# Seven products and an eighth two K-steps later: the sums over partitions of nine conditioning parts, pinned in TensorE's order

## The chip, the cores and the metric

The kernel runs on one core of one Trainium2 chip. The metric is the device time of one execution in microseconds (us), lower is better. The core has TensorE (PE in the profile's rows; PEld is its loading of the stationary operand), VectorE (DVE), ScalarE (ACT), GpSimd (POOL) and SyncE (SP, whose queue starts nearly all loads of weights). Each engine carries out its own instructions in a fixed order, and engines wait for each other through semaphores.

## What is computed

One inference step of a two-layer backbone on 128 context tokens and 128 latent tokens, with a width D of 2048. Layer 0 mixes differential attention and a two-way RWKV-7 scan, layer 1 is a Conformer convolution module, and each layer ends with a ConvFFN. What the change touches is the conditioning: before each block, shift, scale and gate vectors come from a product of the conditioning vector with a 2048 by 12288 matrix per layer.

```python
def adaln(cvec, w, b):
    return (jax.nn.silu(cvec) @ w + b)[:, None, :]

for l in range(DEPTH):
    sh1p, sc1p, g1p, sh2p, sc2p, g2p = jnp.split(adaln(c_ctx[None, :], w_ada[l], b_ada[l]), 6, axis=-1)
    sh1s, sc1s, g1s, sh2s, sc2s, g2s = jnp.split(adaln(c, w_ada[l], b_ada[l]), 6, axis=-1)
    hp = rmsnorm(xp, norm_g[l, 0]) * (1.0 + sc1p) + sh1p
    ...
    xp = xp + g1p * mp
    hp = rmsnorm(xp, norm_g[l, 1]) * (1.0 + sc2p) + sh2p
    xp = xp + g2p * conv_ffn(hp, w_up[l], w_ffn_dw[l], w_down[l])
```

The rows for the latent tokens (xs, hs) are the same with the other vectors.

## The kernel before

**The matrix products.** Activations stand with the channels on the 128 partitions and 256 tokens (both streams) on the free axis, each number split in a high and a low part. A weight matrix is loaded in pieces of 512 KB into one of seven buffers `raw` (`RAW_BUFS`), ACT copies the high part out of it (L192) and DVE or POOL subtracts to get the low part (L194), into one of four slots `wbt`. `gemm` (L235) then runs over groups of output columns and, in each, over K-steps of 128 rows; a K-step with four output tiles is 12 products of 128x128 by 128x256 (L252, L254, L255; L268 to L270 are the same in the last four K-steps of a product that ends a block). After each K-step `gemm` calls a function `fill`, which is where other work is put into the program's order.

**The conditioning** is a Python generator, `ada_gen` (L463), which goes through parts of 1024 columns; each call of `ada_step` takes it to its next `yield`. A part is done in one of two ways. `ada_pe` (L392) multiplies on TensorE: a load of 128 rows by 1024 columns (512 KB, L402) gives four products of 128x32 by 128x256 (L421), one for each quarter j of the columns, and each goes to its own 32 partitions of the tile `ada` (32j to 32j+31). A step of layer 1's parts is two loads and eight products, and a part has eight such steps. `ada_vec` (L426) is used for nine parts, those in `AS_VEC`: DVE multiplies each loaded row block with a scalar and adds it to `av` (L444 and L446), once for each stream s, 32 operations in 32 steps; three idle steps later eight small products with the constant `sel` (L454) sum `av` over the partitions, four quarters j for each of the two streams. Then DVE turns the result (L460), the bias is added (L473), and the part is finished.

**The order of the nine parts** is: layer 0 `g2` (two parts), layer 1 `sc1` (two), `sh1` (two), and `g1` part 0, begun in layer 0's ConvFFN; layer 1 `g2` (two parts) in layer 1's ConvFFN. The parts between them (`g1` part 1, `sc2`, `sh2` of layer 1) are done by `ada_pe` during the convolution block.

**How often steps are taken.** In the two ConvFFNs (`fill0`, `fill2`) a step is taken every second K-step after the sixteenth. Layer 0's ConvFFN has 176 + 88 + 176 + 80 = 520 K-steps, hence 252 steps. In the convolution block (`fill1`) a step is taken every fourth K-step: 32 in its first product (`p_p1`, 144 K-steps), some in the loop after it, 15 in its second product (`p_p2`, 64 K-steps). `ada_until` takes all the steps that are missing at once where a value is needed: for `sh2` of layer 1 that is after `p_p2`, ahead of the second norm of layer 1 (`modulated`, L562, whose instructions are L522, L537, L582, L585 and L587).

**What sets the order.** A scheduler with a simulated timeline puts the program's instructions in order on each engine. It may move an instruction ahead of others on its engine when its operands are ready earlier by its simulation; `tc.keep_in_program_order` takes an instruction out of that.

Of the kernel before, what the change touches and what calls it, by code (L numbers as in the profile page):

```python
# [82 lines left out]
def tile_step(ctx: ExitStack, tc: tile.TileContext, A):  # L83
    nc = tc.nc
    pe, dve, act, pool, sp = nc.tensor, nc.vector, nc.scalar, nc.gpsimd, nc.sync
# [32 lines left out]
    sel = const.tile([P, 2, 32], F32, name="sel")  # L118
# [7 lines left out]
    def bank():  # L126
        return psm[0].tile([P, 512], F32, tag="mm", name="mm")
# [298 lines left out]
    def ada_vec(l, nm, b0, nb):  # L426

        nw = nb * P
        c0 = SEG[nm] * D + b0 * P
        av = nrm_[0].tile([P, 2, 1024], F32, tag="av", name="av", bufs=1)  # L430

        def load(kt):
            raw = rawp.tile([P, 1024], F32, tag="raw", name="raw")
            sp.dma_start(out=raw, in_=A["w_ada"][l, kt * P:(kt + 1) * P, c0:c0 + nw])
            return raw

        nxt = load(0)
        yield
        for kt in range(KT):
            raw, nxt = nxt, (load(kt + 1) if kt < KT - 1 else None)  # L440
            for s in range(2):
                sc = silu_c[:, kt, s:s + 1]
                if kt == 0:
                    dve.tensor_scalar(out=av[:, s], in0=raw, scalar1=sc, scalar2=None, op0=ALU.mult)  # L444
                else:
                    dve.scalar_tensor_tensor(out=av[:, s], in0=raw, scalar=sc, in1=av[:, s], op0=ALU.mult, op1=ALU.add)  # L446
                yield
        for _ in range(3):
            yield
        ps = psa.tile([P, 256], F32, tag="ada", name="ada")  # L450
        for s in range(2):
            rv = av[:, s].rearrange("p (b j c) -> p j b c", j=4, c=32)
            for j in range(4):
                pe.matmul(ps[32 * j:32 * j + 32, 0:nb * 32], lhsT=sel[:, s], rhs=rv[:, j], start=(s == 0), stop=(s == 1))  # L454
        yield
        return ada_turn(ps, nb)

    def ada_turn(ps, nb):
        tr = adap.tile([P, 8, 32], F32, tag="atr", name="atr")
        dve.transpose(out=tr[:, 0:nb].rearrange("p b c -> p (b c)"), in_=ps[:, 0:nb * 32])  # L460
        return tr[:, 0:nb, 0:2]

    def ada_gen():  # L463
        for l, nm, part, parts, b0, nb in ada_order:
            si = SEG[nm]
            if (l, nm, part) in AS_VEC:
                tr = yield from ada_vec(l, nm, b0, nb)
            else:
                tr = yield from ada_pe(l, nm, b0, nb, 2 if l else 1)
            bias = V(f"b_ada{l}", si * KT + b0, nb)  # L470
            av = adaT[:, l * 6 + si, 2 * b0:2 * (b0 + nb)].rearrange("p (b s) -> p b s", s=2)
            eng = pool if l and nm in ("sc2", "sh2") else dve
            eng.tensor_tensor(out=av, in0=tr, in1=bias.unsqueeze(2).to_broadcast([P, nb, 2]), op=ALU.add)  # L473
            if nm in ("sc1", "sc2"):
                ni = 0 if nm == "sc1" else 1
                gvec = V("norm_g", (l * 2 + ni) * KT + b0, nb).unsqueeze(2).to_broadcast([P, nb, 2])
                ac = Acoef[:, l * 2 + ni, b0:b0 + nb]
                if eng is pool:
                    pool.tensor_scalar(out=ac, in0=av, scalar1=1.0, scalar2=None, op0=ALU.add)
                    pool.tensor_tensor(out=ac, in0=ac, in1=gvec, op=ALU.mult)  # L480
                else:
                    dve.scalar_tensor_tensor(out=ac, in0=av, scalar=1.0, in1=gvec, op0=ALU.add, op1=ALU.mult)
            ada_done.add((l, nm, part))
            if part == parts - 1:
                ada_done.add((l, nm))
            yield
# [971 lines left out]
    with ExitStack():  # L1458
# [15 lines left out]
        with scoped("startp", 1) as stp:  # L1474
# [6 lines left out]
            ps = bank()  # L1481
# [13 lines left out]
            with scoped("rowp", 1) as rowp:  # L1495
# [3 lines left out]
                for kt in range(0, KT, 2):  # L1499
                    ps = bank()  # L1500
# [13 lines left out]
        with scoped("nrm1", 2) as nrm_[0]:  # L1514
# [76 lines left out]
            with scoped("cv", 1) as cvp, scoped("cvt", 2) as cvt:  # L1591
# [108 lines left out]
                ps = bank()  # L1700
                first = True
                for ct in list(range(C0, KT)) + [-1]:
# [6 lines left out]
                    for c0, src in srcs:  # L1709
                        for s in range(2):  # L1710
                            pe.matmul(ps[:, c0 + 2 * s:c0 + 2 * s + 2], lhsT=src[:, s * T:(s + 1) * T], rhs=ones[:, 0:2],
                                      start=first, stop=False, skip_group_check=True)
# [103 lines left out]
```

## Time and profile before

| | us |
|---|---|
| median of the three runs | 2710.97 |
| the three runs | 2711.49, 2710.97, 2693.57 |
| the profiled execution, its own time | 2685.66 |
| its span, first to last instruction | 2683.7 |
| mean granted TensorE clock | 0.982 |

The runs shown differ among themselves by 18 us (0.7%), and the profiled execution lies 25 us (0.9%) under the median. Layer 0's ConvFFN fills about 815 to 1565 us of the span, the convolution block 1570 to 1946, and layer 1's ConvFFN the rest.

### The profile page before, as it was taken

Reading aid. Unit: us, or ns where it says so; the run is one execution under the profiler, and the core shown is the slowest. Engines: PE = TensorE matmul, PEld = TensorE weight load, DVE = VectorE, ACT = ScalarE, POOL = GpSimd, SP = SyncE. Lnnn points to the kernel's source line nnn. Section 1 sums busy time; section 2 is a strip of 40 time slices with the busy share of each in tenths; the row PEclk is TensorE's granted clock in tenths of the full one; section 3 lists DMA queues with packets and bytes.
Section 4 is the critical chain, followed back from the end, with each engine's and each line's share of the span. In section 5 each row is a group of like instructions: output and inputs, shape, how many; then the busy total and the mean of one; then the engine's idle time right before and its main releaser. Section 6 shows DMA issues by size and latency. Waiting matters only on the chain.

```text
span 2683.7 us, 60347 instructions
## 1 busy us (share of the span) xinstructions
PE 2590.8 (97%) x24347; PEld 2429.0 (91%) x24347; DVE 2010.5 (75%) x3442; ACT 1258.9 (47%) x2063; POOL 310.7 (12%) x333
## 2 busy tenths in 40 slices
PE   6999998999998999999999989999999999999998
PEld 5898995677998999999999979977989999999998
DVE  3667755766579899888999978985389985566655
ACT  4335544545345444434444454345355453355544
POOL 2000111011100000000000038763300000000000
PEclk9999999999798999999999999999999999999999
DMA  9986666656366888877878857876878876666653
GB/s 301 351 286 191 191 181 238 224 182 222 111 193 190 250 261 256 277 247 249 275 251 265 273 161 229 287 256 205 290 235 278 270 233 194 196 193 193 195 191 118
DMA packets 421368, 616.58 MB, mean 230 GB/s; under 512 B 32437, under 2 KB 291864, under 8 KB 420448
## 3 DMA queue, kind: packets, MB, share of 16 engines
q1 hardware_dynamic: 416688, 600.83, 70.4%
q0 software_dynamic: 3040, 6.57, 0.7%
q10 hardware_dynamic: 1360, 5.33, 0.5%
q8 instruction: 191, 3.13, 0.5%
q14 instruction: 89, 0.73, 0.1%
HBM read 604.75 MB, written 7.86 MB: 228 GB/s over the span
## 4 chain that ended last, share of the span: by engine, by line
PE 83%; DVE 4%; DMA 2%; ACT 1%; issue 1%; SPq 0%; POOL 0%; DVEq 0%; ACTq 0%; POOLq 0%
PE mm L252 23%; PE mm L255 23%; PE mm L254 23%; PE ada L421 3%; DMA raw<-in_w_ada 1%; PE mm L1088 1%; DMA raw<-in_w_up 1%; DVE wbt L194 1%; PE mm L1649 1%; PE mm L1121 1%; PE mm L1125 0%; DVE av L446 0%; PE ada L454 0%; PE mm L1283 0%; PE mm L1292 0%
## 5 line engine op out<-in xcount | busy, mean ns | idle before, releaser
L192 ACT ACTIVATE wbt<-raw 128x1024 fp32r<-128x1024 f32 (+3 forms) x768 | 795.3, 1037 | 1033.1 <-PE mm L254 698.1
L252 PE MATMUL mm<-hbt,wbt 128*128 128x256 f32 x3888 | 1085.0, 282 | 8.5 <-ACT hbt L585 6.4
L194 DVE TENSOR_TENSOR wbt<-raw,wbt 128x1024 fp32r<-128x1024 f32 (+1 forms) x688 | 814.1, 1189 | 359.7 <-ACT wbt L192 349.9
L254 PE MATMUL mm<-hbt,wbt 128*128 128x256 f32 x3888 | 1080.7, 280 | 2.2 <-DVE hbt L587 2.1
L255 PE MATMUL mm<-hbt,wbt 128*128 128x256 f32 x3888 | 1063.1, 280 | 7.5 <-DVE wbt L194 5.4
L252 PEld LDWEIGHTS mm<-hbt,wbt 128*128 128x128 f32 x3888 | 732.7, 189 | 26.5 <-issue 12.5
L254 PEld LDWEIGHTS mm<-hbt,wbt 128*128 128x128 f32 x3888 | 733.8, 189 | 5.9 <-DVE hbt L587 4.4
L255 PEld LDWEIGHTS mm<-hbt,wbt 128*128 128x128 f32 x3888 | 723.3, 189 | 12.3 <-DVE wbt L194 6.7
L254 PE MATMUL mm<-u,wbt 128*128 128x256 f32 x1344 | 371.0, 278 | 0.0
L252 PE MATMUL mm<-u,wbt 128*128 128x256 f32 x1344 | 370.9, 278 | 0.0
L255 PE MATMUL mm<-u,wbt 128*128 128x256 f32 x1344 | 365.7, 278 | 0.0
L446 DVE SCALAR_TENSOR_TENSOR av<-raw,silu_c,av 128x1024 f32<-128x1024 f32 x270 | 337.6, 1279 | 35.3 <-DMA raw<-in_w_ada 35.0
L194 POOL TENSOR_TENSOR wbt<-raw,wbt 128x1024 fp32r<-128x1024 f32 x80 | 194.7, 2440 | 910.0 <-DMA raw<-in_w_pw 805.3
L252 PEld LDWEIGHTS mm<-u,wbt 128*128 128x128 f32 x1344 | 252.2, 188 | 0.4 <-issue 0.4
L254 PEld LDWEIGHTS mm<-u,wbt 128*128 128x128 f32 x1344 | 252.0, 188 | 0.4 <-issue 0.4
L255 PEld LDWEIGHTS mm<-u,wbt 128*128 128x128 f32 x1344 | 249.1, 188 | 0.4 <-issue 0.4
L421 PE MATMUL ada<-raw,silu_c 128*32 128x256 f32 (+2 forms) x2688 | 154.3, 332 | 22.5 <-DMA raw<-in_w_ada 16.6
L1656 DVE SCALAR_TENSOR_TENSOR cu<-mm,vec,cu 128x256 f32<-128x256 f32 x428 | 173.7, 474 | 3.0 <-ACT cu L1640 1.6
L1545 DVE SCALAR_TENSOR_TENSOR cv<-mm,vec,cv 128x254 f32<-128x254 f32 x344 | 147.5, 475 | 12.2 <-ACT cv L1540 12.2
L421 PEld LDWEIGHTS ada<-raw,silu_c 128*32 128x32 f32 x2688 | 68.3, 113 | 74.0 <-issue 26.6
L286 PE MATMUL mm<-hbt,wbt 128*128 128x256 f32 x448 | 131.5, 298 | 0.4 <-ACT hbt L585 0.4
L288 PE MATMUL mm<-hbt,wbt 128*128 128x256 f32 x448 | 126.8, 284 | 0.0
(448 smaller groups left out, 2781.1 us busy)
## 6 DMA issues: line engine op xcount, KB each, us to landing
raw<-in_w_ada SPq DMA_DIRECT2D x384, 512.0 KB, 5.3
raw<-in_w_up SPq DMA_DIRECT2D x688, 256.0 KB, 4.2
raw<-in_w_down SPq DMA_DIRECT2D x168, 512.0 KB, 5.0
raw<-in_w_pw SPq DMA_DIRECT2D x128, 256.0 KB, 4.3
raw<-in_w_in SPq DMA_DIRECT2D x64, 384.0 KB, 5.7
raw<-in_w_in SPq DMA_DIRECT2D x48, 512.0 KB, 3.9
raw<-in_w_out SPq DMA_DIRECT2D x32, 512.0 KB, 3.9
raw<-in_w_pw SPq DMA_DIRECT2D x32, 512.0 KB, 5.4
```

Source lines behind the costliest of these rows:

```text
L192: act.activation(w[:, 0, 0:na * n], v, AF.Copy)
L194: pl.lo(pl.count).tensor_tensor(out=w[:, 1, 0:na * n], in0=v, in1=w[:, 0, 0:na * n].bitcast(F32), op=ALU.subtract)
L252: pe.matmul(ps, lhsT=hi, rhs=r[:, 0:TT], start=(ki == 0 and (nl > 0 or j % 2 == 0)), stop=False, skip_group_check=True)
L254: pe.matmul(ps, lhsT=hi, rhs=r[:, TT:2 * TT], start=False, stop=False, skip_group_check=True)
L255: pe.matmul(ps, lhsT=lo, rhs=r[:, 0:TT], start=False, stop=(ki == nk - 1), skip_group_check=True)
L286: pe.matmul(ps, lhsT=hi, rhs=r[:, 0:TT], start=(ki == 0 and j % 2 == 0), stop=False, skip_group_check=True)
L288: pe.matmul(ps, lhsT=hi, rhs=r[:, TT:2 * TT], start=False, stop=False, skip_group_check=True)
L421: pe.matmul(ps[32 * j:32 * j + 32, 0:nb * 32], lhsT=silu_c[:, kt, :], rhs=rv[:, j], start=(kt == 0), stop=(kt == KT - 1))
L446: dve.scalar_tensor_tensor(out=av[:, s], in0=raw, scalar=sc, in1=av[:, s], op0=ALU.mult, op1=ALU.add)
L1088: pe.matmul(dst_[h][:, s * TT:(s + 1) * TT], lhsT=src[pr, s], rhs=kr[pr, s].rearrange("p a t -> p (a t)"), start=True, stop=True)
L1545: dve.scalar_tensor_tensor(out=o[:, :, a_], in0=v2(ps)[:, :, b_], scalar=w(k, ct), in1=o[:, :, a_], op0=ALU.mult, op1=ALU.add)
L1656: dve.scalar_tensor_tensor(out=o, in0=pads[a](k), scalar=V("w_dw", k * KT + ct), in1=o, op0=ALU.mult, op1=ALU.add)
```

## The change

The eight products that sum `av` over the partitions are no longer issued in one go. First come the four of stream 1 and three of stream 0 (seven together), then the generator yields, and at the next step comes the eighth product, quarter 3 of stream 0, alone. So a part takes one step more than before: 39 steps and not 38. The streams change places (stream 1 starts the sum, stream 0 ends it), and each of the eight products is kept in the program's order on TensorE.

```diff
         ps = psa.tile([P, 256], F32, tag="ada", name="ada")
-        for s in range(2):
+        def add_up(s, js):
             rv = av[:, s].rearrange("p (b j c) -> p j b c", j=4, c=32)
-            for j in range(4):
-                pe.matmul(ps[32 * j:32 * j + 32, 0:nb * 32], lhsT=sel[:, s], rhs=rv[:, j], start=(s == 0), stop=(s == 1))
+            for j in js:
+                ins = pe.matmul(ps[32 * j:32 * j + 32, 0:nb * 32], lhsT=sel[:, s], rhs=rv[:, j], start=(s == 1),
+                                stop=(s == 0))
+                tc.keep_in_program_order(ins)
+
+        add_up(1, range(4))
+        add_up(0, range(3))
+        yield
+        add_up(0, (3,))
         yield
         return ada_turn(ps, nb)
```

In the new file every line behind this place has a number higher by 7, so that L460 is L467 there, L522 is L529, L537 is L544, L582 is L589 and L587 is L594; the two calls of the products share the line L454.

**TensorE, the first of the nine sums, in layer 0's ConvFFN.** Before, all eight stand between products of the ConvFFN:

```order
L252 MATMUL mm<-hbt,wbt 128x256
L254 MATMUL mm<-hbt,wbt 128x256
L255 MATMUL mm<-hbt,wbt 128x256
L454 MATMUL ada<-av,sel 32x256 x8
L255 MATMUL mm<-hbt,wbt 128x256
L252 MATMUL mm<-hbt,wbt 128x256
```

In the new order the first seven:

```order
L254 MATMUL mm<-hbt,wbt 128x256
L255 MATMUL mm<-hbt,wbt 128x256
L454 MATMUL ada<-av,sel 32x256 x7
L252 MATMUL mm<-hbt,wbt 128x256
L254 MATMUL mm<-hbt,wbt 128x256
```

and, 24 products of the ConvFFN (two K-steps) further on, the eighth:

```order
L254 MATMUL mm<-hbt,wbt 128x256
L255 MATMUL mm<-hbt,wbt 128x256
L454 MATMUL ada<-av,sel 32x256
L252 MATMUL mm<-hbt,wbt 128x256
L254 MATMUL mm<-hbt,wbt 128x256
```

The seven stand 140 products of the ConvFFN later than the eight did. The other eight sums have the same form now. Before, five of the nine stood in one piece (this one, the third, fourth, seventh and eighth), three in two pieces of four, and the second in pieces of four, one and three. The seventh stood behind the last product of layer 0's ConvFFN, right ahead of the norm; it now stands 672 products further on, inside `p_p1`, with 48 products between its seven and its eighth.

**DVE, the first norm of layer 1, between layer 0's ConvFFN and the convolution block.** Before:

```order
L511 TENSOR_TENSOR acc<-acc,sq 128x256
L460 STREAM_TRANSPOSE atr<-ada 128x256
L473 TENSOR_TENSOR adaT<-atr,vec 128x16
L529 RECIPROCAL sd<-sd 128x4
L535 TENSOR_SCALAR dg<-table,sd 128x128
L582 SCALAR_TENSOR_TENSOR mm<-x_7807,Acoef,mm 128x128 x2
L587 SCALAR_TENSOR_TENSOR hbt<-mm,adaT,hbt 128x128 x2
```

and now:

```order
L518 TENSOR_TENSOR acc<-acc,sq 128x256
L536 RECIPROCAL sd<-sd 128x4
L542 TENSOR_SCALAR dg<-table,sd 128x128
L589 SCALAR_TENSOR_TENSOR mm<-x_7807,Acoef,mm 128x128
L446 SCALAR_TENSOR_TENSOR av<-raw,silu_c,av 128x1024 x2
L589 SCALAR_TENSOR_TENSOR mm<-x_7807,Acoef,mm 128x128
L594 SCALAR_TENSOR_TENSOR hbt<-mm,adaT,hbt 128x128 x2
```

The end of the seventh part (L460, L473) is gone from here; two of its DVE operations stand between the first two operations of the norm, and four more (not shown) ahead of and among the first group's convolution in `p_p1`. The load that feeds the two is in SP's order behind nine pieces of the `p_p1` weights, the first of which are already split by POOL.

**TensorE, the second norm of layer 1, between `p_p2` and layer 1's ConvFFN.** Before:

```order
L270 MATMUL mm<-hbt,wbt 128x256
L421 MATMUL ada<-raw,silu_c 32x256 x24
L522 MATMUL mm<-ones,acc 128x2
L522 MATMUL mm<-ones,sq 128x2
L522 MATMUL mm<-ones,acc 128x2
L522 MATMUL mm<-ones,sq 128x2
L537 MATMUL mm<-dg,ones 128x256
L252 MATMUL mm<-hbt,wbt 128x256 x2
```

and now:

```order
L270 MATMUL mm<-hbt,wbt 128x256
L421 MATMUL ada<-raw,silu_c 32x256 x28
L529 MATMUL mm<-ones,acc 128x2
L529 MATMUL mm<-ones,sq 128x2
L529 MATMUL mm<-ones,acc 128x2
L529 MATMUL mm<-ones,sq 128x2
L421 MATMUL ada<-raw,silu_c 32x256 x8
L544 MATMUL mm<-dg,ones 128x256
L421 MATMUL ada<-raw,silu_c 32x256 x4
L252 MATMUL mm<-hbt,wbt 128x256 x2
L421 MATMUL ada<-raw,silu_c 32x256 x4
L254 MATMUL mm<-hbt,wbt 128x256
```

Before, 24 conditioning products (six loads) were left for this place; now it is 64 (sixteen loads, all of the second part of `sh2`). Three more groups of four and one of eight follow behind the rows shown, among the products of the first four K-steps; the last eight have 48 products of the ConvFFN ahead of them.

**SP at the same place.** Before:

```order
L603 DMA raw<-in_w_pw 128x2x512
L606 DMA raw<-in_w_up 128x2x256 x2
L402 DMA raw<-in_w_ada 128x1024 x2
L606 DMA raw<-in_w_up 128x2x256 x2
L402 DMA raw<-in_w_ada 128x1024 x4
L606 DMA raw<-in_w_up 128x2x256 x20
```

and now:

```order
L402 DMA raw<-in_w_ada 128x1024 x2
L610 DMA raw<-in_w_pw 128x2x512
L613 DMA raw<-in_w_up 128x2x256 x4
L402 DMA raw<-in_w_ada 128x1024 x16
L613 DMA raw<-in_w_up 128x2x256 x20
```

Two pieces of the ConvFFN's weights (two issues each) stand ahead of the conditioning loads in both; the third stands behind four of them before, and behind all sixteen now.

## The prediction

> **What bounds the kernel now.** I read the page's totals and chain first, then the table of windows over the stages that hold the nine sums, then TensorE's waits.
>
> ```profile
> span 2683.7 us, 60347 instructions
> PE 2590.8 (97%) x24347; PEld 2429.0 (91%) x24347; DVE 2010.5 (75%) x3442; ACT 1258.9 (47%) x2063; POOL 310.7 (12%) x333
> ...
> PE 83%; DVE 4%; DMA 2%; ACT 1%; issue 1%; SPq 0%; POOL 0%; DVEq 0%; ACTq 0%; POOLq 0%
> ...
> 900.00:980.00 80.00, 80.00 (x688) 79.28 (x687) 71.04 (x92) 38.48 (x56) 0.00 (x0) 1.00 0.80 247
> 1320.00:1400.00 80.00, 80.00 (x686) 78.91 (x685) 74.20 (x97) 39.12 (x57) 0.00 (x0) 1.00 0.81 256
> 1700.00:1740.00 40.00, 40.00 (x365) 37.13 (x364) 38.43 (x99) 15.29 (x18) 31.12 (x17) 1.00 0.87 284
> ...
> PE mm L255 <- DVE wbt L194: 2.3, 3, 1.0
> ```
>
> TensorE has 83% of the chain. The windows give busy us of PE, PEld, DVE, ACT and POOL, then clock, DMA share and GB/s: in both ConvFFNs' stages PE is busy throughout, DVE nearly so. The last row is all that PE waited in layer 0's ConvFFN from 860 to 1540 us. So the price of a small product there is what it takes out of PE's stream.
>
> **The eighth product alone.** Three places of PE's timeline show what a sum costs when it stands whole, as one product, and as three (each product has two records, so x16, x2 and x6).
>
> ```profile
> 914.02 0.28 PE L255 MATMUL mm<-hbt,wbt 128*128 128x256 f32 x1
> 914.23 1.07 PE L454 MATMUL ada<-av,sel 128*32 128x256 f32 x16
> 915.23 0.39 PE L255 MATMUL mm<-hbt,wbt 128*128 128x256 f32 x1
> 915.45 0.28 PE L252 MATMUL mm<-hbt,wbt 128*128 128x256 f32 x1
> ...
> 1029.05 0.28 PE L255 MATMUL mm<-hbt,wbt 128*128 128x256 f32 x1
> 1029.26 0.62 PE L454 MATMUL ada<-av,sel 128*32 128x256 f32 x2
> 1029.81 0.39 PE L255 MATMUL mm<-hbt,wbt 128*128 128x256 f32 x1
> 1030.03 0.28 PE L252 MATMUL mm<-hbt,wbt 128*128 128x256 f32 x1
> 1030.15 0.28 PE L254 MATMUL mm<-hbt,wbt 128*128 128x256 f32 x1
> ...
> 1040.23 0.28 PE L255 MATMUL mm<-hbt,wbt 128*128 128x256 f32 x1
> 1040.44 0.63 PE L454 MATMUL ada<-av,sel 128*32 128x256 f32 x6
> 1041.00 0.39 PE L252 MATMUL mm<-hbt,wbt 128*128 128x256 f32 x1
> 1041.22 0.28 PE L254 MATMUL mm<-hbt,wbt 128*128 128x256 f32 x1
> ```
>
> From the last large product before to the second after it, less the two ordinary steps (1030.03 to 1030.15 is one; 0.117 each, 0.235 together): eight take 1.43 - 0.235 = 1.20 us, one takes 0.98 - 0.235 = 0.75, three take 0.99 - 0.235 = 0.76. So one product costs what three cost (four quarters run side by side, and the way in and out is paid once a group), and the second four add only 0.44. Seven are two rounds, as eight are: 1.20. The new form costs 1.20 + 0.75 = 1.95 a part.
>
> Before, by the order: the parts 1, 3, 4 and 8 whole (4 x 1.20), the parts 5, 6 and 9 in two fours (3 x 1.52, a four priced as a three), the second in three pieces (2.27), which is 11.6 us; the seventh stood in the gap ahead of the norm and counts nothing. Now eight parts are in the ConvFFNs, 8 x 1.95 = 15.6. **Term 1: +4.0 us.** PE hides none of it. The later place of the sums costs nothing: `av` is ready, and who waits for the result is a norm or a residual many K-steps on.
>
> **What a step more does.** Layer 0's ConvFFN has 252 steps. Six parts take 6 x 38 = 228, which left 24 for the seventh; now 6 x 39 = 234 leave 18. So six DVE operations of the seventh part, its sum, and with them all later parts slip by seven steps into the convolution block.
>
> In `p_p1` the conditioning runs in groups of eight products, four K-steps apart; a group is the same shape as the eight above, 1.20 us. By the order five groups fewer stand in `p_p1` (14, not 19), the same number in the loop after it and in `p_p2`; the five stand at the second norm now. That takes 5 x 1.20 = 6.0 out of PE's stream and puts the seventh sum, 1.95, into it. **Term 2: -4.05 us.** DVE gets four more operations there:
>
> ```profile
> L446 DVE SCALAR_TENSOR_TENSOR av<-raw,silu_c,av 128x1024 f32<-128x1024 f32 x270 | 337.6, 1279 | 35.3 <-DMA raw<-in_w_ada 35.0
> ...
> DVE mm L1632 <- ACT cg L1628: 19.5, 7, 5.9
> ```
>
> 4 x 1.28 = 5.1 us. I cost them at nothing, since DVE waits 19.5 us from 1600 to 1860 us for ACT's sigmoid, which itself waits for PE's products. If that cover is gone (the window 1700 to 1740 has 38.43 us of DVE in 40), PE's gain is lost and up to 5.1 come on top.
>
> **The first norm of layer 1.** The other two operations stand between the first two of the norm's (L582), on the path by which PE starts again.
>
> ```profile
> 1564.72 7.21 POOL L194 TENSOR_TENSOR wbt<-raw,wbt 128x1024 fp32r<-128x1024 f32 x3 [3.42 <-ACT wbt L192]
> ...
> 1573.38 0.74 DVE L582 SCALAR_TENSOR_TENSOR mm<-x,Acoef,mm 128x128 f32<-128x128 f32 x2 [1.38 <-PE mm L537]
> ...
> L434 SPq DMA_DIRECT2D raw<-in_w_ada x144: 328/340/1829, 744.3 to 2160.7; - x144
> ...
> DMA to landing us min/median/max: 3.5/5.0/6.9
> ```
>
> Their load follows nine weight pieces on SP, and it waits for a buffer that POOL's third split of `p_p1` releases. That is the second of the three in the row, which ends at about 1564.72 + 2/3 x 7.21 = 1569.5. It lands 3.5 to 5.0 us later, at 1573.0 to 1574.5; then come 2 x 1.28. The second L582 began at 1573.77 and would begin at about 1577. **Term 3: +3 us**, from 0 (if the next chunks catch up) to 8 (landing in 6.9, and DVE held while POOL works).
>
> **The second norm of layer 1.** Sixteen loads where there were six.
>
> ```profile
> 1945.63 0.28 PE L270 MATMUL mm<-hbt,wbt 128*128 128x256 f32 x1
> 1945.84 2.80 PE L421 MATMUL ada<-raw,silu_c 128*32 128x256 f32 x48
> ...
> 1954.12 1.22 PE L537 MATMUL mm<-dg,ones 128*128 128x256 f32 x2 [3.62 <-ACT dg L534]
> 1956.51 0.58 PE L252 MATMUL mm<-hbt,wbt 128*128 128x256 f32 x1 [1.16 <-ACT hbt L585]
> ...
> 1958.41 0.41 PE L254 MATMUL mm<-hbt,wbt 128*128 128x256 f32 x1
> 1958.62 0.41 PE L255 MATMUL mm<-hbt,wbt 128*128 128x256 f32 x1
> ...
> 1965.61 0.28 PE L252 MATMUL mm<-hbt,wbt 128*128 128x256 f32 x1
> ...
> 1880.00:1900.00 20.00, 20.00 (x191) 18.07 (x184) 8.38 (x16) 7.70 (x10) 7.02 (x5) 1.00 0.91 310
> ...
> DMA to landing us min/median/max: 3.5/5.5/10.7
> ```
>
> Call 1945.84 the zero: `p_p2` is done, and seven loads can stand in the seven buffers. The first product frees a buffer at about 0.5; the eighth load lands at 4, the others follow at 0.52 MB / 310 GB/s = 1.7 us, so the sixteenth at about 4 + 8 x 1.7 = 17.6. PE's start of the ConvFFN (1956.51) is at 10.7; the first K-steps run at steps of 0.21 (1958.41 to 1958.62), and the 48 products ahead of the last eight take until 21 or later. So the loads come in time, if closely, and the 28 and 8 ahead of L537 lie in the gap, where PE waited anyway. What stays are the five groups among the first K-steps, 5 x 0.75 = 3.7 us, and about 1 us for the split of the third weight piece, which DVE now makes behind L460. K-step 4, at 1965.61 before, moves by 4.7. **Term 4: +4.7 us**, from 0 to 8.5 (the groups at the half-speed steps).
>
> The 48 products from 1956.51 to 1965.61 take 9.1 us, where 48 ordinary steps of 0.117 take 5.6: the slow steps of 0.21 behind the gap cost 3.5, over some 7 us. The Trainium skill, TensorE: Matmul & The Clock Gate, Part 1 (the HAM clock gate), says that PE's clock halves after an idle window of about 3.4 us and is back after one busy window of that length; the trace agrees in kind, but its slow steps last twice as long. By that rule the twelve conditioning products which now stand between L522 and the first K-step could keep the clock up.
>
> **The sum:** 4.0 - 4.05 + 3 + 4.7 = +7.6 us, on the profiled execution's 2685.66 it gives 2693.3. The runs' median is 25 us higher; on 2710.97 it gives 2719, which I predict. The bounds: 4.0 - 4.05 + 0 + 0 = 0, and 4.0 + (1.95 + 5.1) + 8 + 8.5 = +27.
>
> **Rivals.**
> Loads one by one at the second norm (the other side): if the nine loads behind the first seven did not overlap and came 5.5 us apart (the median landing), the last would land at 4 + 8 x 5.5 = 48, 27 us after PE wants it, and the time would be 2711 + 7.6 + 27 = 2746. It decides once they come more than about 4.5 us apart, (21 + 19 - 4) / 8, since 7.6 and 19 make 1%. Against it: SP issues them freely, and 310 GB/s were held in `p_p2` with two kinds of loads at once.
> DVE as the bound of `p_p1`: the gain of term 2 is lost and 5.1 added, so +7.6 + 4.05 + 5.1 = +17, or 2728. For it speaks 38.43 of 40; against it the 19.5 us of waits.
> The clock stays up at the second norm: with products in the gap PE may start K-step 0 at full speed, which takes those 3.5 us off: +4.1, or 2715, inside the forecast's own range. For it speaks that the gap of 3.6 us ahead of L537 gets eight products, against it that they take 1.2 us of it.
> Everything moved is hidden: terms 3 and 4 are nothing, since PE idles in both gaps, and terms 1 and 2 cancel: 2711. For it speaks that PE does nothing from 1950 to 1954; against it that the groups stand behind 1956.
> The change does something else than its name: in the order all nine sums have the new form, but the seventh is not two K-steps long but four, and no product stands where PE would have waited. Nothing comes of this.
>
> **Chances.** The forecast (2713 to 2724, with the case of the clock, 0.1 of it) 0.52; all hidden (within 2 us) 0.20; DVE as the bound (2724 to 2736) 0.18; loads one by one 0.07; a gain that I don't see 0.03. The range is from 2693, the fastest run shown with a sum of zero, to 2737, the median with the upper bound: no less, as the runs shown spread over 18 us themselves. It leaves out the last two cases and little more. A change of 1% (27 us) is about what a measurement of this kernel can tell from none. Faster by that: 0.03. Slower: the loads one by one, and a tail of DVE's case, 0.09. Within 1%: 0.88.
>
> **What would show it.** L454 in groups of x14 and x2 with 0.75 us for the x2; nine times. In `p_p1` the groups of L421 begin some 28 K-steps later, with PE still busy throughout; a PE that waits there for DVE shows the second rival. The two L446 between the first L582 rows, with a wait for the load ahead of them; none shows term 3 wrong. At the second norm the last L421 ends at about 23 after `p_p2`, with waits for in_w_ada of a microsecond or so in all; waits of several us each show the first rival. A sum outside 0 to 27 on like runs shows that I missed a place.

## The result: slower by 0.76%, and where the time went

Over 16 runs each, the kernel before took 2693.21 us (2683.76 to 2714.09) and the changed one 2718.81 us (2712.33 to 2721.76). The ratio is 1.0076, with a 95% interval from 1.0055 to 1.0096: some 20 us slower by the ratio and 25.6 between the medians, less than 1%. The forecast of 2719 us met the time by luck, not by its own reasons. Two of the three runs that it was put on were among the high ones of the kernel before: of the 107 runs of that kernel in this study 76 lie under 2704 us, and the other 31 between 2705 and 2720. For the profiled execution the forecast added 7.6 us; the spans of the two profiled executions differ by 33.2, outside the 0 to 27 that the prediction allowed its sum.

The page of the changed kernel has the same number of instructions on PE, DVE, ACT and POOL; PE is busy 32.5 us longer.

```profile
span 2716.9 us, 60367 instructions
...
PE 2623.3 (97%) x24347; PEld 2454.8 (90%) x24347; DVE 2005.8 (74%) x3442; ACT 1260.2 (46%) x2063; POOL 312.6 (12%) x333
...
PE 83%; DVE 3%; DMA 3%; issue 2%; ACT 1%; SPq 0%; POOL 0%; POOLq 0%; DVEq 0%; ACTq 0%
```

To see where, number the large products (`L252`, `L254`, `L255` and their like, 17952 in both traces) in their order, and take the start of each product before from its start now:

```
product   before    after   difference  since the row above   what lies between
   3600    862.8    863.7    +0.95
   9450   1563.9   1565.0    +1.14      +0.2   layer 0's ConvFFN, six sums
   9900   1638.8   1642.9    +4.09      +2.95  first norm of layer 1
  10950   1792.3   1790.4    -1.91      -6.0   p_p1
  11100   1857.2   1862.5    +5.27      +7.2   end of p_p1, convolution
  11700   1937.5   1942.4    +4.94      -0.3   p_p2
  11850   1970.4   1979.5    +9.18      +4.2   second norm of layer 1
  end of the span           +33.2       +24.0  layer 1's ConvFFN
```

Up to 1970 us the edit costs 8.2, about what the sum said. The other 24 us arise in layer 1's ConvFFN, where only the eighth and the ninth sum stand. The windows (busy us and instructions of PE, PEld, DVE, ACT, POOL, then granted clock, DMA share, GB/s) show it without any sum in them. Two windows of the kernel before:

```profile
2100.00:2170.00 70.00, 70.00 (x597) 70.00 (x596) 69.22 (x86) 34.57 (x49) 0.00 (x0) 1.00 0.86 269
2300.00:2400.00 100.00, 100.00 (x884) 100.00 (x884) 60.41 (x81) 46.73 (x61) 0.00 (x0) 1.00 0.65 195
```

and one of the changed kernel:

```profile
2300.00:2400.00 100.00, 100.00 (x851) 100.00 (x850) 55.90 (x76) 42.74 (x52) 0.00 (x0) 1.00 0.60 187
```

PE is full and its granted clock 1.00 in all three, yet 100 us hold 884 products before and 851 now. TensorE has two steps (a step is the time from one large product's start to the next one's): 0.1133 or 0.1178 us (150 of them take 17.0 or 17.67). The kernel before itself ran at the slow one from 2076 to 2180 us (597 in 70 us). Its rows at the ninth sum show the switch (start, us, engine, line; x8 is four products):

```profile
2180.77 0.28 PE L254 MATMUL mm<-hbt,wbt 128*128 128x256 f32 x1
2180.89 0.28 PE L252 MATMUL mm<-hbt,wbt 128*128 128x256 f32 x1
2181.01 0.28 PE L254 MATMUL mm<-hbt,wbt 128*128 128x256 f32 x1
2181.21 0.64 PE L454 MATMUL ada<-av,sel 128*32 128x256 f32 x8
2181.78 0.39 PE L255 MATMUL mm<-hbt,wbt 128*128 128x256 f32 x1
2182.01 0.28 PE L252 MATMUL mm<-hbt,wbt 128*128 128x256 f32 x1
2182.13 0.28 PE L254 MATMUL mm<-hbt,wbt 128*128 128x256 f32 x1
...
2184.34 0.64 PE L454 MATMUL ada<-av,sel 128*32 128x256 f32 x8
2184.91 0.39 PE L255 MATMUL mm<-hbt,wbt 128*128 128x256 f32 x1
2185.13 0.28 PE L252 MATMUL mm<-hbt,wbt 128*128 128x256 f32 x1
2185.24 0.28 PE L254 MATMUL mm<-hbt,wbt 128*128 128x256 f32 x1
```

Up to the second four the steps are 0.12, behind it 0.11, and so they stay until 2663 us, for 4217 products. At the changed kernel's ninth sum (x14 are seven, x2 is the eighth) they are 0.12 before and behind:

```profile
2208.42 1.06 PE L454 MATMUL ada<-av,sel 128*32 128x256 f32 x14
2209.41 0.39 PE L252 MATMUL mm<-hbt,wbt 128*128 128x256 f32 x1
2209.64 0.28 PE L254 MATMUL mm<-hbt,wbt 128*128 128x256 f32 x1
2209.76 0.28 PE L255 MATMUL mm<-hbt,wbt 128*128 128x256 f32 x1
...
2212.44 0.62 PE L454 MATMUL ada<-av,sel 128*32 128x256 f32 x2
2212.99 0.39 PE L252 MATMUL mm<-hbt,wbt 128*128 128x256 f32 x1
2213.21 0.28 PE L254 MATMUL mm<-hbt,wbt 128*128 128x256 f32 x1
2213.33 0.28 PE L255 MATMUL mm<-hbt,wbt 128*128 128x256 f32 x1
```

From 1970 us on the kernel before had 5148 fast steps, the changed one next to none: 5148 x 0.0045 = 23.2 us, and the two sums' direct price is 1.2 more (3.9 in place of 1.20 + 1.52). That makes 24.4, the 24 of the table. Of it 4.2 us lie between the second norm and the eighth sum, a stretch that two of the experiments below show slow without a split sum ahead of it.

### The profile page after: what moved, and what is told of

Its sections match the earlier page's. It is cut to its first block, busy times and chain, and to the rows that moved or that the text cites. A ratio compares the mean times of both kernels' runs of the same rounds, so it can differ in the third digit from the quotient of the medians.

```text
span 2716.9 us, 60367 instructions
## 1 busy us (share of the span) xinstructions
PE 2623.3 (97%) x24347; PEld 2454.8 (90%) x24347; DVE 2005.8 (74%) x3442; ACT 1260.2 (46%) x2063; POOL 312.6 (12%) x333
## 4 chain that ended last, share of the span: by engine, by line
PE 83%; DVE 3%; DMA 3%; issue 2%; ACT 1%; SPq 0%; POOL 0%; POOLq 0%; DVEq 0%; ACTq 0%
PE mm L252 23%; PE mm L255 23%; PE mm L254 23%; PE ada L421 3%; DMA raw<-in_w_ada 2%; PE mm L1095 1%; PE mm L1656 1%; DVE wbt L194 1%; PE mm L1128 1%; PE ada L454 1%; PE mm L1132 0%; DVE av L446 0%; DMA raw<-in_w_up 0%; PE mm L1290 0%; PE mm L1224 0%
## 5 line engine op out<-in xcount | busy, mean ns | idle before, releaser
L192 ACT ACTIVATE wbt<-raw 128x1024 fp32r<-128x1024 f32 (+3 forms) x768 | 794.9, 1037 | 1054.2 <-PE mm L254 702.7
L252 PE MATMUL mm<-hbt,wbt 128*128 128x256 f32 x3888 | 1089.4, 283 | 10.0 <-ACT hbt L592 7.6
L254 PE MATMUL mm<-hbt,wbt 128*128 128x256 f32 x3888 | 1082.9, 281 | 1.5 <-DVE hbt L594 1.3
L255 PE MATMUL mm<-hbt,wbt 128*128 128x256 f32 x3888 | 1060.7, 280 | 7.3 <-DVE wbt L194 4.8
L252 PEld LDWEIGHTS mm<-hbt,wbt 128*128 128x128 f32 x3888 | 731.4, 189 | 31.0 <-issue 15.0
L254 PEld LDWEIGHTS mm<-hbt,wbt 128*128 128x128 f32 x3888 | 732.4, 188 | 6.7 <-DVE hbt L594 4.4
L255 PEld LDWEIGHTS mm<-hbt,wbt 128*128 128x128 f32 x3888 | 721.5, 189 | 8.8 <-DVE wbt L194 5.6
L252 PE MATMUL mm<-u,wbt 128*128 128x256 f32 x1344 | 374.9, 280 | 0.0
L254 PE MATMUL mm<-u,wbt 128*128 128x256 f32 x1344 | 373.5, 279 | 0.0
L255 PE MATMUL mm<-u,wbt 128*128 128x256 f32 x1344 | 369.7, 279 | 0.0
L252 PEld LDWEIGHTS mm<-u,wbt 128*128 128x128 f32 x1344 | 252.2, 188 | 1.6 <-issue 1.6
L254 PEld LDWEIGHTS mm<-u,wbt 128*128 128x128 f32 x1344 | 251.4, 187 | 0.0
L255 PEld LDWEIGHTS mm<-u,wbt 128*128 128x128 f32 x1344 | 250.4, 188 | 0.0
L421 PE MATMUL ada<-raw,silu_c 128*32 128x256 f32 (+2 forms) x2688 | 158.5, 336 | 27.4 <-DMA raw<-in_w_ada 20.8
L421 PEld LDWEIGHTS ada<-raw,silu_c 128*32 128x32 f32 x2688 | 68.3, 114 | 81.1 <-issue 27.6
```

The source lines that it names most:

```text
L192: act.activation(w[:, 0, 0:na * n], v, AF.Copy)
L252: pe.matmul(ps, lhsT=hi, rhs=r[:, 0:TT], start=(ki == 0 and (nl > 0 or j % 2 == 0)), stop=False, skip_group_check=True)
L254: pe.matmul(ps, lhsT=hi, rhs=r[:, TT:2 * TT], start=False, stop=False, skip_group_check=True)
L255: pe.matmul(ps, lhsT=lo, rhs=r[:, 0:TT], start=False, stop=(ki == nk - 1), skip_group_check=True)
L421: pe.matmul(ps[32 * j:32 * j + 32, 0:nb * 32], lhsT=silu_c[:, kt, :], rhs=rv[:, j], start=(kt == 0), stop=(kt == KT - 1))
```

## The experiments

The theory after the result: a small group can switch TensorE between its two steps, the step then holds until the next group, and the new form of the ninth sum no longer switches it to the fast one. The rivals: only the prices of the sum count; the slip by seven K-steps makes the last stage slow; the lone product does. In the experiments' files the lines move by a few: `L454` is also `L457` or `L459`, and the large products are also `L253`, `L255`, `L256`, `L257`, `L258`, `L260`.

**The new form for the ninth part alone** (last_part_new; the lines are added to the changed kernel, and give the other eight sums their old form).

```diff
+        if (l, nm, b0) != (1, "g2", 8):
             for s in range(2):
...
+            yield
+            return ada_turn(ps, nb)
+        def add_up(s, js):
```

> The kernel before, with the new form (seven, and the eighth two K-steps later) for the ninth part alone; the eight other sums, and with them everything up to layer 1's ConvFFN, stay as before. Theory of the pace: after every small group TensorE settles on one of two steps, 0.1133 or 0.1178 us a product, and keeps it until the next group; the ninth part's second group of four set it to 0.1133 for the last 480 us (4217 products) in most runs of the kernel before, and the single product leaves it at 0.1178. Then the profile shows 0.1178 from the ninth sum to the end, every run loses the fast end: about 2690 + 4217 x 0.0045 = 2709, no run under 2700. Theory of the sum of prices: 1.95 in place of 1.52, +0.4 us, and runs spread as those of the kernel before, most of them from 2684 to 2697.

Measured: 2710.43 us (2704.51 to 2718.71, 12 runs) beside 2695.56 of the kernel before, ratio 1.004 (1.0014 to 1.0065). The profile runs slow from the ninth sum to the end:

```profile
2300.00:2400.00 100.00, 100.00 (x852) 100.00 (x851) 56.24 (x76) 42.88 (x52) 0.00 (x0) 1.00 0.62 186
```

Against the kernel before, each 150 products behind the sum lose 0.67 us, in all 16 us from product 14100 to 17700. So one sum whose own price differs by 0.4 us makes 15 of the 25 us between the medians. The rival that only the prices of the sum count falls. The stretch between the second norm and the eighth sum, fast in the kernel before (975 steps, 4.4 us), was slow in this profile and in the next, where nothing of the split stands ahead of it; so its being slow in the changed kernel can't be put down to the split.

**The K-step more, without the split** (step_only; added to the kernel before).

```diff
                     pe.matmul(ps[32 * j:32 * j + 32, 0:nb * 32], lhsT=sel[:, s], rhs=rv[:, j], start=(s == 0), stop=(s == 1))
         yield
+        yield
```

> The kernel before with nothing but the one K-step more for each part (no split, nothing pinned): parts slip by seven steps as in the changed kernel, the eighth part's sum stands whole and the ninth's in two fours, as before. Theory of the pace: the ninth part's second four sets the step to 0.1133 in about two runs of three, so the runs fall into two clusters some 20 us apart, the lower one at 2684 to 2697 plus 3.6 us for the terms 2 to 4, less up to 1: about 2687 to 2700. Rival, that the slip itself makes the last stage slow (more transfers or VectorE work beside it): every run at 2712 or above, with 0.1178 after the ninth sum. Sum of prices: +3 us, one cluster's shape as before.

Measured: 2695.82 us (2689.19 to 2702.19, 12 runs), ratio 0.9989 (0.9965 to 1.0013). The slip costs at most 3.5 us by this interval (the runs of the kernel before hold high ones, and these don't; beside its 22 runs under 2704, with a median of 2694.1, the slip costs 1.7), and the last stage is fast behind the ninth sum's second four:

```profile
2300.00:2400.00 100.00, 100.00 (x885) 100.00 (x884) 59.66 (x82) 45.83 (x58) 0.00 (x0) 1.00 0.65 195
```

The slip as the cause falls. The upper cluster that I expected in a third of the runs did not show in twelve; why is open.

**The lone product away** (eight_step).

```diff
         add_up(1, range(4))
-        add_up(0, range(3))
+        add_up(0, range(4))
         yield
-        add_up(0, (3,))
         yield
```

> The changed kernel with all eight products of a sum together, pinned, and the K-step after them left as it is; so only the lone product goes. Sum of prices: eight parts in the ConvFFNs less 0.75 each, -6.0 us against the changed kernel's 2718.8, so 2713. Theory of the pace: groups of eight always left the slow step, so it stays 0.1178 from the ninth sum to the end, also 2713 and nothing near 2695. Rival, that the lone product is what makes the last stage slow: 2690 to 2697.

Measured: 2714.2 us (2710.82 to 2725.38, 10 runs), ratio 1.0062 (1.0032 to 1.0092). The step is slow from 857 us to the end in the profile, but for a few us, and so in the last stage:

```profile
2300.00:2400.00 100.00, 100.00 (x852) 100.00 (x851) 56.32 (x76) 42.77 (x52) 0.00 (x0) 1.00 0.62 187
```

The lone product is not what makes it slow, only what fails to end it; its price, 4.6 us between the medians where 6.0 was expected, is not resolved by the intervals.

**Other splits: five and three, four and four** (five_three, four_four).

```diff
-        add_up(0, range(3))
+        add_up(0, range(1))
         yield
-        add_up(0, (3,))
+        add_up(0, range(1, 4))
```

```diff
         add_up(1, range(4))
-        add_up(0, range(3))
         yield
-        add_up(0, (3,))
+        add_up(0, range(4))
```

> The changed kernel with the eight products of a sum as five and, two K-steps later, three, in place of seven and one, at all nine parts. The direct price is that of seven and one (two rounds 1.20 us, one round 0.76), so the sum of prices gives 2719, as the changed kernel. Theory of the pace: groups of two rounds always left 0.1178; groups of four products that met the slow step left 0.1133 in four of six cases, single ones in one of nine. If three behave like four, the step is 0.1133 after about two sums of three: up to 24 us less in layer 0's ConvFFN and 23 in layer 1's, in all about 2685 to 2700. If three behave like one: 2719 and 0.1178 throughout.

> The changed kernel with each sum as four products and, two K-steps later, the other four, pinned as the new form is. Sum of prices: 1.52 in place of 1.95 at eight parts, -3.4 us, so 2715. Theory of the pace: the first four turns 0.1178 to 0.1133 in most cases and the second turns it back (0.1133 became 0.1178 at every group seen so far), so most parts end slow and about one in four fast: some 10 us less than the sum, 2700 to 2710, with runs spread over 20 us by the ninth part's outcome.

Measured: 2717.97 us (2713.3 to 2725.82), ratio 1.0074 (1.0049 to 1.0099), and 2720.71 us (2716.16 to 2732.07), ratio 1.0085 (1.0056 to 1.0114). With five and three all sums end slow. With four and four the first four switched to the fast step at two of nine parts, and each time the second four took it back; no second four switched. So the number of products in the last group does not decide, and my chance of two in three, taken from six cases, was wrong. What differed from the kernel before was the distance between the two groups: 24 large products here, 20 there.

**Another place of the eighth product: 25, 26, 27 behind the seven** (late_25, late_26, late_27). A hook in the loop over a K-step's products issues it; for 26:

```diff
                     pe.matmul(ps, lhsT=hi, rhs=r[:, TT:2 * TT], start=False, stop=False, skip_group_check=True)
+                    while j == 0 and late:
+                        late.pop(0)()
...
-        add_up(0, (3,))
+        late.append(lambda: add_up(0, (3,)))
         yield
```

> The changed kernel with the eighth product two large products later: 26 stand between the seven and it, not 24 (it comes between the second and the third product of a tile); nothing else in TensorE's order moves. In the profiles so far a single, three or four that met the slow step 20 or 44 products after the group before it left the fast step in five cases of five, and after 24 or 48 in none of 27. Theory of the pace with a phase of three products (20, 44 and 26 leave 2 when divided by 3; 24 and 48 leave 0): the step is 0.1133 after each sum, up to 24 us less in layer 0's ConvFFN and 23 in layer 1's, 2675 to 2690, faster than both kernels, and fast ones only. If what counted was another count than three, or chance: 2719 as the changed kernel, or some sums fast. Sum of prices: 2719.

> The changed kernel with the eighth product one large product later, 25 behind the seven (between the first and the second product of a tile, which use the same weights). With a phase of three products this is the count that has not been seen behind a slow group with certainty (it leaves 1): fast or slow, but the same at all sums. If any place inside a tile gives the fast step: 0.1133 behind each sum and 2675 to 2690. Sum of prices: 2719.

> The changed kernel with the eighth product three large products later, 27 behind the seven, on a tile's boundary as in the changed kernel but inside a K-step. Phase of three: as 24, the slow step 0.1178 behind every sum and 2719. If the place inside the K-step is what counts: as 26, 2675 to 2690. Sum of prices: 2719.

Measured: late_26 2715.63 us, ratio 1.0061 (1.0032 to 1.0091); late_25 2719.62, 1.0064 (1.0038 to 1.0091); late_27 2719.36, 1.0066 (1.0035 to 1.0098). All 27 sums end slow. The phase of three falls, and a place inside a tile is not enough.

**Twenty products between the groups** (late_20 with seven and one, four_20 with two fours). The first group is issued from the hook four products into the next K-step; the edit of four_20:

```diff
+                    while j == 1 and late:
+                        late.pop(0)()
...
-        add_up(1, range(4))
-        add_up(0, range(3))
+        def first():
+            add_up(1, range(4))
+
+        late.append(first)
         yield
-        add_up(0, (3,))
+        while late:
+            late.pop(0)()
+        add_up(0, range(4))
```

> The changed kernel with the seven products moved four large products into the next K-step, so that 20 (19 at two parts) and not 24 large products stand between them and the eighth. If the count between two groups decides (20 gave the fast step four times of four in the kernel before and two of the experiments), the profile shows 0.1133 after most sums and 2675 to 2695. If it is not the count: 0.1178 throughout and 2712 to 2722.

> As the one before it with two fours in place of seven and one. If the count decides: 0.1133 after most sums, 2675 to 2690. If it doesn't: some of the fours that meet the slow step turn it, by the cases so far about one in four where the group stands at a K-step's start: 0.1178 after most sums, 2705 to 2720.

Measured: one run each, 2732.58 and 2684.03 us. With seven and one all sums end slow at 19, 20 and 44 products (its first sum began 14 us later than the changed kernel's, before anything of this edit acts, so that its time is not read). With two fours the second one switches to the fast step where the distance is 20 or 44 (five sums) and does not at 18 or 19 (three); at one part the first four had switched, and the second took it back. It is not the number in the last group: in the kernel before, and in last_part_new, the second sum's lone product, 20 behind a four, switched to the fast step. So at such short distances both count: the group ahead must be one round of products, four or fewer, and the distance must fit. What switches a first four, some 700 to 1000 products behind the group ahead, is not shown.

**The same, timed, and with the second four inside a K-step** (four_20_timed, four_20_inside). The second:

```diff
+                    if j == 2 and late:
+                        late[0][0] -= 1
+                        if late[0][0] == 0:
+                            late.pop(0)[1]()
...
         add_up(1, range(4))
-        add_up(0, range(3))
+        late.append([2, lambda: add_up(0, range(4))])
         yield
-        add_up(0, (3,))
+        while late:
+            late.pop(0)[1]()
         yield
```

> The kernel of the look before (two fours, 20 large products between them at five of the eight parts in the ConvFFNs, 18 or 19 at three, 44 at the seventh), now timed. Theory of the pace with the count: a four that meets the slow step 20 or 44 products after another four turns it to 0.1133, at 18, 19, 24, 28 or 48 it does not; so the ninth part ends fast in nearly every run and the first, third and sixth mostly, and the runs lie at 2678 to 2700, median near 2687, below both kernels. If the one look was luck: a median near 2715 with runs spread over 30 us.

> Two fours again, the first at the K-step's boundary as in the run with 24, the second 20 products later at all parts but the sixth (there as three and one), which now puts it inside a K-step, between the second and third product of a tile. If the count decides wherever the group stands: 0.1133 after the second four of most parts, and 2675 to 2695. If the place counts with it: 0.1178 throughout and 2712 to 2722, as with 24.

Measured: 2690.15 us (2682.54 to 2700.29, 12 runs), ratio 0.9969 (0.9944 to 0.9994), and 2683.25 us (2677.14 to 2692.59, 12 runs), ratio 0.9941 (0.9916 to 0.9965), beside 2693.77 of the kernel before. The second beats both kernels, with the same arithmetic: by 10 us the kernel before, measured beside it, and by 35 the changed one's median of 2718.81. Its ninth sum:

```profile
2192.26 0.28 PE L260 MATMUL mm<-hbt,wbt 128*128 128x256 f32 x1
2192.37 0.28 PE L253 MATMUL mm<-hbt,wbt 128*128 128x256 f32 x1
2192.48 0.28 PE L255 MATMUL mm<-hbt,wbt 128*128 128x256 f32 x1
2192.60 0.28 PE L260 MATMUL mm<-hbt,wbt 128*128 128x256 f32 x1
2192.80 0.64 PE L459 MATMUL ada<-av,sel 128*32 128x256 f32 x8
2193.37 0.39 PE L253 MATMUL mm<-hbt,wbt 128*128 128x256 f32 x1
2193.59 0.28 PE L255 MATMUL mm<-hbt,wbt 128*128 128x256 f32 x1
2193.71 0.28 PE L260 MATMUL mm<-hbt,wbt 128*128 128x256 f32 x1
...
2195.93 0.64 PE L459 MATMUL ada<-av,sel 128*32 128x256 f32 x8
2196.49 0.39 PE L260 MATMUL mm<-hbt,wbt 128*128 128x256 f32 x1
2196.72 0.28 PE L253 MATMUL mm<-hbt,wbt 128*128 128x256 f32 x1
2196.83 0.28 PE L255 MATMUL mm<-hbt,wbt 128*128 128x256 f32 x1
```

The first four ends a fast stretch (0.34 for three steps before it, 0.12 for one behind), the second starts the next, which holds to 2662 us. Here all five second fours that came 20 products after a slow first one switched; at three parts the first had switched and the second took it back. The sixth sum stands in three pieces and ends slow.

## Why the forecast came out as it did

- **The step that failed** is one the forecast never wrote down as a step: it took 0.117 us for every ordinary product, in both kernels, and priced only what is put into or taken out of that stream. The step itself depends on the groups. Its own rows hold both: those from 1030.15 to 1040.23 lay in a fast stretch (89 steps in 10.08 us, 0.1133 each), its windows of 900 to 980 and 1320 to 1400 in slow ones but for 3 us. The term that it lacks is 23 us on the profiled executions, three times the sum. That 2719 met the time is luck, owed to the high runs in the median of three: on this result's median of 2693.21 the sum gives 2700.8, 18 us short.
- **Term 1, +4.0:** the prices were right. In the changed kernel seven take 1.19 and the eighth 0.75 at all nine parts, worked out as the prediction did it. But layer 0's ConvFFN gained only 0.2 where 2.8 of the term lay. PE's waits for split weights fell with it, from the 2.3 us in three waits that the prediction quotes to this one, and products that start late beside the waits fell too:

```profile
PE mm L255 <- DVE wbt L194: 0.4, 1, 0.4
```

- **Term 2, -4.05:** the five groups leave `p_p1` and the stretch gains 6.0, but the end of `p_p1` and the convolution give 7.2 back, so +0.9 net with `p_p2`. The rival had a loss of the gain, but with DVE as the bound in `p_p1`; DVE has more room there than before (36.35 us of 40 busy in the window 1700 to 1740 below, 38.43 before). Instead PE waits 8.6 us from 1780 to 1870 where it waited 6.0, mostly for conditioning loads and for ACT, and the granted clock is lower. The windows before:

```profile
1830.00:1860.00 30.00, 26.30 (x198) 22.03 (x197) 20.30 (x46) 19.34 (x39) 9.73 (x8) 0.89 0.45 150
```

and now:

```profile
1700.00:1740.00 40.00, 40.00 (x377) 35.69 (x376) 36.35 (x96) 13.64 (x16) 28.62 (x14) 1.00 0.91 299
...
1830.00:1860.00 30.00, 24.90 (x170) 19.94 (x168) 15.99 (x41) 16.16 (x32) 7.46 (x6) 0.77 0.43 137
```

  By an estimate from these rows, a clock lower by 0.12 over 30 us is some 3.6 us.
- **Term 3, +3:** right in size (2.95) and place, wrong in its cause. The two operations stand between the norm's first two and take 2.47 us, but the load was in time: no wait stands at their row.

```profile
1574.57 0.36 DVE L589 SCALAR_TENSOR_TENSOR mm<-x,Acoef,mm 128x128 f32<-128x128 f32 x1 [1.37 <-PE mm L544]
1574.83 2.47 DVE L446 SCALAR_TENSOR_TENSOR av<-raw,silu_c,av 128x1024 f32<-128x1024 f32 x2
1577.22 0.35 DVE L589 SCALAR_TENSOR_TENSOR mm<-x,Acoef,mm 128x128 f32<-128x128 f32 x1
```

- **Term 4, +4.7:** +4.2. The sixteen loads came in time, with two waits for them of 1.0 us in all; the split of the third weight piece cost 1.9 where I had put 1. PE's waits from 1945 to 1992 us in the changed kernel:

```profile
PE mm L255 <- DVE wbt L194: 1.9, 2, 1.0
PE ada L421 <- DMA raw<-in_w_ada: 1.0, 2, 0.6
```

- **The rivals.** Loads one by one: fallen. All hidden: fallen. The clock that stays up: in part. The clock fell all the same, but the slow steps of 0.21 last from 1961.62 to 1963.93 (2.3 us) where before they lasted from 1957.60 to 1963.32 (5.7 us). Over the ordinary steps they cost 2.7 us before, not the 3.5 that the prediction took, and 1.1 now; that is in term 4's +4.2. The granted clock stood at 0.50 from 1953.11 to 1963.35 before and from 1957.09 to 1963.92 now.
- **Why the kernel before has high runs** is argued only. If its ninth sum's first four happens to switch, the second takes it back, and the stretch costs 19 us, the distance between the clusters. No profile caught such a run.

## What to carry to other kernels

Before pricing an edit by what it puts into TensorE's stream, count the large products in equal windows on both sides of each interruption: a step that differs by 4% over thousands of products outweighs every inserted instruction. Small groups between large products are best judged by the step that they leave behind, and two clusters among the runs of one kernel, 20 us apart here, may come of such a step (argued here, not shown). If a sum can be cut, try several distances and keep the one whose profile ends fast.

## What the runs showed of the hardware

TensorE ran the same products at 0.1133 or 0.1178 us at a granted clock of 1.00, and the step changed only at an interruption. A wait can be one too: in late_25 TensorE waited 0.76 us for a split weight at 1238.9 us and went on at 0.1133, and in four_20 it waited 1.3 at 1200 and went on at 0.1178. The groups of conditioning products, over the 14 profiles, from 860 us on and where some seven steps on each side are undisturbed: a group that met the fast step left the slow one, 29 times of 29; a group of two rounds (five to eight products, those of `L421` included) that met the slow step left the slow one, 354 of 354; a group of one round that met the slow step behind another of one round left the fast one at a distance of 20 or 44 large products, 19 of 19, and the slow one at 18, 19, 24, 28 or 48, 15 of 15; behind a group of two rounds, 19 to 51 products away, it left the slow one, 55 of 55. Two kinds of place show that this is no full rule. At 672 to 1037 products behind the group ahead, fours that met the slow step left the fast one 12 times and the slow one 29 times. And of the fours of `L421` among the first K-steps behind the second norm, 12 or 18 products behind the one ahead and with shorter stretches to read, 3 of 18 left the fast step. Many of these are the same place in kernels that differ little, so they are fewer independent cases than they look. Why 20 and 44 fit is open.

The restart does not tell what will follow. At the kernel before's ninth sum the first two large products behind the first four start 0.227 us apart, behind the second, which switches, 0.223; but behind the changed kernel's first seven they start 0.221 apart, and the step stays slow.

The Trainium skill, TensorE: Matmul & The Clock Gate, Part 2 (Back-to-back issue gap), gives one gap at full clock for 256 columns, 262 cycles or 0.109 us by its formula, as that of an isolated product, and says that in a stream with weight loads both operations set the spacing. The traces show two steps in such a stream, 0.1133 and 0.1178, and there the measurement decides.

The granted clock fell at the second norm without a long gap. In the changed kernel no wait of PE there exceeds 0.61 us (the first row), and yet (windows as above):

```profile
1954.19 0.64 PE L421 MATMUL ada<-raw,silu_c 128*32 128x256 f32 x8 [0.61 <-DMA raw<-in_w_ada]
...
1954.00:1958.00 4.00, 3.46 (x33) 1.94 (x34) 0.46 (x2) 0.67 (x2) 0.00 (x0) 0.89 0.99 356
1958.00:1962.00 4.00, 3.78 (x21) 1.29 (x20) 3.30 (x13) 1.92 (x7) 0.00 (x0) 0.50 1.02 406
```

Groups of small products keep PE busy in the records, but did not hold the clock here. The Trainium skill, TensorE: Matmul & The Clock Gate, Part 1 (the HAM clock gate), has it fall after an idle window of about 3.4 us; by PE's records there was none.
